# A two-layer hybrid encoder on one core: norm weights written as rows, norms turned two blocks at a time, and other places for the last MLP weights

## The chip, the core and the metric

The kernel runs on one core of a Trainium2 chip. The metric is the device time of one execution in microseconds; the median of three runs of the kernel before is 1523.51 us (1521.68 to 1525.11). One execution was profiled: it took 1525.2 us, with a span of 1523.4 us and a mean granted TensorE clock of 0.97. The engines are called as in the profile: PE (TensorE), DVE (VectorE), ACT (ScalarE), POOL (GpSimd), and SP, which here only issues DMAs.

## The reference

Two layers work on `x` of 512 x 1024 float32. Each layer mixes the tokens, then applies an MLP, both between two norms. Six vectors per layer (`shift`, `scale`, `gate`, twice) come from one vector `c` by a product with 1024 x 6144 weights:

```python
mod = (cond @ mod_w + mod_b)[:, None, :]
shift1, scale1, gate1, shift2, scale2, gate2 = jnp.split(mod, 6, axis=-1)
h = rms_norm(x, attn_pre_g) * (1.0 + scale1) + shift1
proj = h @ w_in
...
y = jnp.concatenate([y_a, y_b, y_c, y_d], axis=-1) @ w_out
x = x + gate1 * rms_norm(y, attn_post_g)
h = rms_norm(x, mlp_pre_g) * (1.0 + scale2) + shift2
y = jnp.square(jax.nn.relu(h @ mlp_w1)) @ mlp_w2
return x + gate2 * rms_norm(y, mlp_post_g)
```

The mixers (sparse attention, retention, gated linear attention, differential attention) are not touched by the change.

## The kernel before

**Products.** Each product of two matrices is made of three matmuls (`mm3`, L267 to L271): operands are split in a high part, rounded, and a low part, the rest. `prep` (L255 to L266) does so for a tile of weights: a DMA on SP's queue loads 256 KB into one of four `raw` buffers (L261), ACT casts the high part `whi` (L263), and DVE or POOL subtracts for the low part `wlo` (L265). Strings in the table `PLAN` say which of the two does it, letter by letter (`d` or `p`): `blo` for the first three weight groups of layer 1, `wolo` for the out-projection's, `w1lo` for the MLP's first hidden weights. `slots` is a list of pools that take the tiles in turn.

**Order.** The program is written as one stream; a scheduler sorts the instructions of each engine, and each engine then works in its order. A DMA waits in the order of the queue that issues it.

**Modulation vectors.** `gemv` (L279 to L282) loads 512 KB into one of two `gw` buffers by SP's queue and lets DVE multiply and sum them (1.2 us). Those of the MLP part of layer 0 and all of layer 1 (56 steps) are spread over the MLP of layer 0 by `fill`: one with each hidden tile, two with each output tile. `gain` (L304) makes of such a vector the 128 x 8 weights of a norm. The norms behind the projections need them as a row that is the same on all 128 partitions: `gain_row` (L488 to L495) writes the 128 x 8 tile to memory in the order of a row, four bytes at a time (L493, `rows<-g_post`), and reads it back to all partitions (L494, `row_post<-rows`), both on SP's queue. There are four such rows in the program.

**Rest of a layer** (`rest`, L1236 to L1363). Tokens go in four blocks of 128. The out-projection does 48 matmuls for each block (`po`); then `add_block` (L497) multiplies by the row, takes the mean of squares (`rsqrt_mean`, L467 to L483: two ACT squares, five short DVE steps, two short ACT steps) and updates x; `norm_block` (L505) norms the new x with another mean and two ACT multiplications (L511); and `turn_block` (L514 to L529) turns the normed block: eight PE transposes (L522) into two PSUM buffers, eight ACT evictions of 128x128 that apply scale and shift (L525), the cast `h_h` (L527), and on DVE the low part `h_l` (L528). The turn of a block stands behind the matmuls of the next one; that of block 3 behind the fourth hidden tile of the MLP. The MLP runs in four quarters q: eight hidden tiles `pf` of 24 matmuls (in q = 0 in two halves of 256 tokens each), squared into `hd` by `hidden` (ACT, DVE, a cast and a low part), then eight output tiles `p` of 24 matmuls. In the last quarter the output runs block by block, both halves of a block in a row, and each block is then added, normed and turned for the next layer.

**Transition.** The first weight groups of layer 1 (groups 3, 0 and 1, each of four tiles; L751 to L768) are applied block by block: `ptm` matmuls, of group 3 first; blocks 0 and 1 can go while blocks 2 and 3 are still normed, and `ch()`, the turn of block 3, is called at group 1 of block 1. ACT copies the results out of PSUM (`tK`, `Va`, `wi`, `ca`, L720 to L723; `tI`, L746). The four blocks of x are saved by DMAs of ACT's queue (L1347) and read back in the next out-projection.

Of the kernel before, what the change touches and what calls it, by code (L numbers as in the profile page):

```python
# [24 lines left out]
 'blo': 'dppd',  # L25
# [53 lines left out]
 'w1lo': 'dp',  # L79
 'wm': 12,  # L80
 'wolo': 'pdpddppp',
# [117 lines left out]
def tile_trunk(ctx: ExitStack, tc: tile.TileContext, a, out, dbg=None):  # L199
# [55 lines left out]
    def prep(src, shape, lo_eng=None):  # L255
        n = cnt[0]
        cnt[0] += 1
        pl, th, tl, bufs = slots[0]
        slots.append(slots.pop(0))
        raw = wp.tile(shape, F32, name=f"raw{n}", tag="raw", bufs=PLAN["rb"])  # L260
        sp.dma_start(raw, src)  # L261
        hi = pl.tile(shape, F32R, name=f"whi{n}", tag=th, bufs=bufs)
        act.copy(hi, raw)  # L263
        lo = pl.tile(shape, F32R, name=f"wlo{n}", tag=tl, bufs=bufs)
# [202 lines left out]
    def rsqrt_mean(halves, name):  # L467

        ss = tiny("ss" + name, 2)
        for c in range(2):  # L470
            junk = nt.tile([P, T], F32, name=f"jk{name}{c}", tag="nm_r", bufs=1)
            act.activation(junk, halves[c], AF.Square, accum_out=ss[:, c:c + 1])
# [32 lines left out]
    def norm_block(x, name):  # L505

        r = rsqrt_mean([x[:, hs(c)] for c in range(2)], name)
        xn = []
        for c in range(2):
            xn.append(nt.tile([P, T], F32, name=f"xn{name}{c}", tag="rs", bufs=RS))  # L510
            act.mul(xn[c], x[:, hs(c)], r)  # L511
        return xn
# [873 lines left out]
```

## Time and profile before

| | |
|---|---|
| median of three runs | 1523.51 us (1521.68 to 1525.11) |
| the profiled execution | 1525.2 us, span 1523.4 us |
| mixers of layer 0, out-projection, MLP, transition | to about 335, 390, 782, 833 us of the span |
| mixers of layer 1, out-projection, MLP | to about 1095, 1150, 1516 us |
| from the last matmul to the end | 7.6 us |
| DMA packets, and of these under 512 B | 83,094 and 13,188 |

Times are counted from the start of the span. A row of the timeline has its start, its length, engine, line, operation and output<-input; in brackets stands how long the engine was idle before it and what it waited for. A row of the waits has the waiting engine and line, the engine and line waited for, the total in us, how often, and the longest. A row of stretches has start:end, the width, and busy us of PE, its weight loads, DVE, ACT and POOL with their instructions, then the granted clock of TensorE, the DMA share and GB/s. A group's row has the instructions, busy us and mean ns, and the idle time ahead of them.

### The profile page before, as it was taken

How to read it: one execution, taken by the hardware profiler on the slowest of the kernel's cores; microseconds unless marked ns; L12 is line 12 of the kernel's file. 1: busy time of each engine (PE TensorE's matmuls, PEld its weight loads, DVE VectorE, ACT ScalarE, POOL GpSimd, SP SyncE). 2: the span in 40 equal slices, each digit the busy share in tenths (PEclk: the TensorE clock that was granted, in tenths of full speed). 3: DMA queues.
4: the chain of work that ended last, by engine and by line, in shares of the span. 5: the costliest groups of instructions: out<-in, count | busy, mean ns of one | idle time of the engine just before them, and what ended most of it. 6: DMA issues, size and time to landing. Idle time of an engine off the chain costs nothing.

```text
span 1523.4 us, 21884 instructions
## 1 busy us (share of the span) xinstructions
PE 1420.2 (93%) x7730; PEld 1148.0 (75%) x7730; DVE 947.6 (62%) x2119; ACT 759.0 (50%) x1739; POOL 250.7 (16%) x234
## 2 busy tenths in 40 slices
PE   8889889998899959999978989999988999999998
PEld 4576868766898838888868868787568988888886
DVE  8898978774674766525464989764555434254444
ACT  4577476565742312414465765856657444142331
POOL 3343421332100000000022344213330000000000
PEclk8999999999999969999999999999999999999999
DMA  9531222453287876524132102211331443142311
GB/s 345 189 93 42 84 70 84 147 185 112 64 278 192 276 214 206 131 63 125 56 117 71 37 28 78 76 43 42 120 113 59 111 123 93 62 130 82 107 42 56
DMA packets 83094, 173.13 MB, mean 114 GB/s; under 512 B 13188, under 2 KB 15910, under 8 KB 82728
## 3 DMA queue, kind: packets, MB, share of 16 engines
q1 hardware_dynamic: 82084, 169.59, 36.7%
q10 hardware_dynamic: 900, 2.14, 0.4%
q8 instruction: 61, 1.00, 0.3%
q14 instruction: 49, 0.40, 0.1%
HBM read 167.48 MB, written 4.21 MB: 113 GB/s over the span
## 4 chain that ended last, share of the span: by engine, by line
PE 70%; DVE 15%; ACT 6%; issue 4%; DMA 4%; POOL 1%; SPq 0%; ACTq 0%; DVEq 0%; POOLq 0%
PE p L271 8%; PE p L269 8%; PE p L270 8%; PE pf L269 7%; PE pf L270 7%; PE pf L271 7%; PE ptm L269 3%; PE ptm L270 3%; PE ptm L271 3%; DMA gw<-modw 3%; DVE ia L814 2%; DVE m L813 2%; ACT whi L263 1%; DVE ia L800 1%; PE ptc_t L271 1%
## 5 line engine op out<-in xcount | busy, mean ns | idle before, releaser
L263 ACT CAST whi<-raw 128x512 fp32r<-128x512 f32 x388 | 236.5, 621 | 336.6 <-PE p L271 120.7
L265 POOL TENSOR_TENSOR wlo<-raw,whi 128x512 fp32r<-128x512 f32 x122 | 161.3, 1342 | 751.8 <-ACT whi L263 707.5
L265 DVE TENSOR_TENSOR wlo<-raw,whi 128x512 fp32r<-128x512 f32 x266 | 184.0, 703 | 150.3 <-ACT whi L263 147.0
L270 PE MATMUL pf<-h_l,whi 128*128 128x512 f32 (+1 forms) x640 | 223.3, 349 | 0.0
L269 PE MATMUL pf<-h_h,whi 128*128 128x512 f32 (+1 forms) x640 | 223.3, 351 | 0.0
L271 PE MATMUL pf<-h_h,wlo 128*128 128x512 f32 (+1 forms) x640 | 223.0, 349 | 0.0
L269 PE MATMUL ptm<-whi,h_h 128*128 128x256 f32 x592 | 176.7, 299 | 10.0 <-ACT ca L723 6.8
L270 PE MATMUL ptm<-wlo,h_h 128*128 128x256 f32 x592 | 173.3, 293 | 0.9 <-POOL wlo L265 0.9
L271 PE MATMUL ptm<-whi,h_l 128*128 128x256 f32 x592 | 172.3, 291 | 0.0
L282 DVE CUSTOM_DVE_ANT_0 gw<-gw,cond 128x1024 f32<-128x1024 f32 x80 | 101.6, 1273 | 65.2 <-DMA gw<-modw 64.9
L269 PEld LDWEIGHTS pf<-h_h,whi 128*128 128x128 f32 x640 | 121.4, 191 | 16.9 <-ACT h_h L527 0.2
L271 PEld LDWEIGHTS pf<-h_h,wlo 128*128 128x128 f32 x640 | 121.1, 189 | 16.8
L270 PEld LDWEIGHTS pf<-h_l,whi 128*128 128x128 f32 x640 | 121.1, 189 | 16.7
L269 PEld LDWEIGHTS ptm<-whi,h_h 128*128 128x128 f32 x592 | 116.1, 196 | 18.4 <-issue 7.3
L270 PEld LDWEIGHTS ptm<-wlo,h_h 128*128 128x128 f32 x592 | 116.7, 197 | 6.3 <-issue 4.8
L271 PEld LDWEIGHTS ptm<-whi,h_l 128*128 128x128 f32 x592 | 116.5, 197 | 1.8 <-issue 1.5
L270 PE MATMUL po<-wlo,yT_h 128*128 128x512 f32 x128 | 51.8, 404 | 2.9 <-POOL wlo L265 2.9
L813 DVE MAX8 m<-ia 128x8 f32<-128x256 f32 (+2 forms) x96 | 53.2, 555 | 1.3
L269 PE MATMUL po<-whi,yT_h 128*128 128x512 f32 x128 | 52.8, 412 | 0.2 <-ACT yT_h L446 0.2
L814 DVE MATCH_REPLACE8 ia<-m,ia 128x256 f32<-128x256 f32 (+2 forms) x96 | 51.9, 541 | 0.0
L271 PE MATMUL po<-whi,yT_l 128*128 128x512 f32 x128 | 51.2, 400 | 0.6 <-DVE yT_l L447 0.6
L917 ACT COPY QF<-q 32x256 f32<-32x256 f32 x120 | 48.4, 403 | 5.2 <-DVE q L894 2.2
(418 smaller groups left out, 3028.4 us busy)
## 6 DMA issues: line engine op xcount, KB each, us to landing
raw<-w SPq DMA_DIRECT2D x256, 256.0 KB, 2.8
gw<-modw SPq DMA_DIRECT2D x80, 512.0 KB, 4.3
raw<-wtm SPq DMA_DIRECT2D x76, 256.0 KB, 2.8
gs<-modw SPq DMA_DIRECT2D x16, 512.0 KB, 7.5
raw<-wo SPq DMA_DIRECT2D x32, 256.0 KB, 2.8
raw<-wtc SPq DMA_DIRECT2D x24, 256.0 KB, 2.8
xin<-xT SPq DMA_DIRECT2D x8, 256.0 KB, 3.5
wq<-wtm SPq DMA_DIRECT2D x8, 256.0 KB, 5.7
```

The costliest lines, as they stand in the source:

```text
L263: act.copy(hi, raw)
L265: (lo_eng or dve).tensor_tensor(lo, raw, bits(hi), ALU.subtract)
L269: pe.matmul(ps, l[0], r[0], start=start, stop=False)
L270: pe.matmul(ps, l[0], r[1], start=False, stop=False)
L271: pe.matmul(ps, l[1], r[0], start=False, stop=stop)
L282: return dve.tensor_tensor_reduce(raw, raw, cond, 1.0, 0.0, ALU.mult, ALU.add, modT[l][:, c:c + 1])
L800: e.scalar_tensor_tensor(t, rl, wi[:, b, hd:hd + 1], t, ALU.mult, ALU.add)
L813: dve.max(m8, acc)
L814: dve.match_replace(acc, m8, acc, MARK)
L917: f(Q[r, :, hd, :], QS4[c // 2][r, 2 * (c % 2):2 * (c % 2) + 2, :])
```

## The change

Four things change.

1. **Rows.** The weights of the norm behind a projection are made as soon as their modulation vector is there (`gain_out`): PE turns the 128 x 8 tile to 8 x 128, ACT copies it out of PSUM, and a DMA of POOL's queue writes it as eight contiguous pieces. The read to all partitions, and the saves of x, also go to POOL's queue.
2. **Norms and turns.** x is normed by one ACT square of 128x1024 and one DVE scaling of 128x1024, written in the place of the block's output tile. Two blocks are turned at once (`turn_half`): 4 x 4 transposes, evictions of 128x256, by turns ACT's and DVE's. Blocks 0 and 1 are turned behind the first half of block 3's out-projection, blocks 2 and 3 behind the sixth hidden tile. In the last quarter of layer 0 the output runs (0,0), (0,1), (1,0), (1,1), (2,1), (3,1), then the turn of blocks 0 and 1, then (2,0), (3,0), each a block and a half of the columns; the turn of blocks 2 and 3 is called at group 1 of block 1, as block 3's was.
3. **Weights.** Of the last MLP weights the eight of the second half of the columns (`wr`) lie in the place of the MLP's input `h2`, which is read until the last hidden tile. The first weights of layer 1 take other slots.
4. **Low parts.** `blo`, `w1lo` and `wolo` give more of them to DVE: 34 of POOL's 122 in the program, 14 in each out-projection and its MLP's start, 6 at the transition.

```diff
- 'blo': 'dppd',
+ 'blo': 'dddd',
- 'w1lo': 'dp',
+ 'w1lo': 'd',
- 'wolo': 'pdpddppp',
+ 'wolo': 'ppdddddd',
...
+                    if part in (2, 5):
+                        gain_out(l, "post1" if part == 2 else "post2")
...
+    def gain_out(l, which):
+        gain(l, which)
+        pt = tr.tile([P, T], F32, name=f"tg_{which}{l}", tag="tr")[0:KT, 0:P]
+        pe.transpose(pt, gmul[l, which], ident)
+        g = nt.tile([P, T], F32, name=f"gt_{which}{l}", tag="sq")[0:KT, 0:P]
+        act.copy(g, pt)
+        pool.dma_start(rows[2 * l + (which == "post2")], g)
     def gain_row(l, which):
-        sp.dma_start(d.rearrange("k p -> p k"), g)
-        sp.dma_start(row, d.rearrange("k p -> (k p)").unsqueeze(0).broadcast_to([P, DM]))
+        pool.dma_start(row, d.rearrange("k p -> (k p)").unsqueeze(0).broadcast_to([P, DM]))
...
+    def norm_block(x, xn, name):
+        ss = tiny("ss" + name)
+        f = xn.rearrange("p c t -> p (c t)")
+        square(ss, x, f)
+        dve.tensor_scalar(f, x, rsqrt_mean(ss, name), None, ALU.mult)
+        return f
+    def turn_half(l, which, sh_part, hf, xn, parts, name):
...
+        for c in range(4):
...
+            for i in range(2):
+                for b in range(2):
+                    k = 2 * c + i
+                    pe.transpose(pt[:, i, P * b:P * b + P], xn[2 * hf + b][:, P * k:P * k + P], ident)
+            for i in range(2):
+                k = 2 * c + i
+                if i:
+                    act.activation(v[:, i], pt[:, i], AF.Identity, scale=g[:, k:k + 1], bias=sh[:, k:k + 1])
+                else:
+                    dve.tensor_scalar(v[:, i], pt[:, i], g[:, k:k + 1], sh[:, k:k + 1], ALU.mult, ALU.add)
...
-            if b:
-                turn(b - 1)
+                if (b, c) == (NB - 1, 0):
+                    turn(0)
...
-                    if (q, half, f) == (0, 0, 3):
-                        turn(NB - 1)
+                    if (q, half, f) == (0, 0, 5):
+                        turn(1)
...
+        wr = h_tiles(f"wr{l}_")
+        ws = [[prep(a["w2"][l, 3, 0, k], [P, T]) for k in range(KT)],
+              [prep(a["w2"][l, 3, 1, k], [P, T], place=wr[k]) for k in range(KT)]]
+        last = [(0, 0), (0, 1), (1, 0), (1, 1)]
+        last += [(2, 1), (3, 1), (2, 0), (3, 0)] if l + 1 < L else [(2, 0), (2, 1), (3, 0), (3, 1)]
...
-                act.dma_start(xsave[b], x)
-                xn[b] = norm_block(x, f"p1n{l}_{b}")
+                pool.dma_start(xsave[b], x)
+                xn[b] = norm_block(x, y[b], f"p1n{l}_{b}")
```

How the order moves, at three places. On TensorE, at the end of layer 0's out-projection, the order before has the last matmuls of block 3 (`po_3_1`), the first four transposes of block 2 (`txp_20`) and then the MLP's first hidden tiles (`pf`):

```order
L270 MATMUL po_3_1_4395<-wlo_4041,yT_h 128x512
L271 MATMUL po_3_1_4395<-whi_4039,yT_l 128x512
L522 MATMUL txp_20_4420<-ident,xnpn_20_4366 128x128 x4
L269 MATMUL pf_0_0_0_4510<-h_h,whi_4500 128x256
L269 MATMUL pf_0_1_0_4552<-h_h,whi_4542 128x256
```

With the change the transposes of blocks 0 and 1 (`txp_00` to `txp_03`, out of the output tile `yo_m`) stand between the halves of block 3:

```order
L274 MATMUL po_3_0_4304<-whi_3993,yT_l 128x512
L538 MATMUL txp_00_4329<-ident,yo_m 128x128 x4
L538 MATMUL txp_01_4339<-ident,yo_m 128x128 x4
L272 MATMUL po_3_1_4369<-whi_3999,yT_h 128x512
L273 MATMUL po_3_1_4369<-wlo_4000,yT_h 128x512
L274 MATMUL po_3_1_4369<-whi_3999,yT_l 128x512
L272 MATMUL po_3_1_4369<-whi_4005,yT_h 128x512
L273 MATMUL po_3_1_4369<-wlo_4006,yT_h 128x512
L274 MATMUL po_3_1_4369<-whi_4005,yT_l 128x512
L538 MATMUL txp_02_4349<-ident,yo_m 128x128 x4
```

So the transposes of a block that was just normed are gone from there, and no transpose stands between the out-projection and the first hidden tiles. On SP's queue, in the MLP of layer 0, the order before has the write of a row among the loads of MLP weights (`raw<-w`) and modulation weights (`gw`):

```order
L261 DMA raw_6023<-w 128x512
L280 DMA gw_3_2_6117<-modw 128x1024
L261 DMA raw_6029<-w 128x512
L493 DMA rows<-g_post_11548 128x8x1
L280 DMA gw_3_3_6120<-modw 128x1024
L261 DMA raw_6035<-w 128x512
```

With the change the same loads follow one another:

```order
L259 DMA raw_6001<-w 128x512
L283 DMA gw_3_2_6089<-modw 128x1024
L259 DMA raw_6007<-w 128x512
L283 DMA gw_3_3_6092<-modw 128x1024
L259 DMA raw_6013<-w 128x512
```

The write has gone to POOL's queue, behind a transpose and a copy. On ACT, at the transition, the order before has block 3's normed halves (`xnp1n_30`, `xnp1n_31`) ahead of the copies of group 3's result for block 0 (`Va`, `wi`, `ca` out of `ptm_3_0`):

```order
L478 ACTIVATE rsp1n_3_7784<-rsp1n_3_7784 128x1
L263 CAST whi_7864<-raw_7862 128x512
L263 CAST whi_7870<-raw_7868 128x512
L720 COPY tK_0_7884<-ptm_3_0_7892 128x128
L511 ACTIVATE xnp1n_30_7791<-x_3_4046,rsp1n_3_7784 128x512
L511 ACTIVATE xnp1n_31_7793<-x_3_4046,rsp1n_3_7784 128x512
L721 COPY Va_7880<-ptm_3_0_7892 128x64
L722 ACTIVATE wi_7881<-ptm_3_0_7892 128x8
L723 COPY ca_7882<-ptm_3_0_7892 128x16
```

With the change these copies, of blocks 0 and 1, come ahead of block 3's square (`ym_1_5060, ssp1n_3`):

```order
L739 COPY tK_0_7788<-ptm_3_0_7796 128x128
L740 COPY Va_7784<-ptm_3_0_7796 128x64
L267 CAST whi_7750<-raw_7748 128x512
L741 ACTIVATE wi_7785<-ptm_3_0_7796 128x8
L742 COPY ca_7786<-ptm_3_0_7796 128x16
L267 CAST whi_7756<-raw_7754 128x512
L739 COPY tK_1_7789<-ptm_3_1_7825 128x128
L740 COPY Va_7784<-ptm_3_1_7825 128x64
L741 ACTIVATE wi_7785<-ptm_3_1_7825 128x8
L742 COPY ca_7786<-ptm_3_1_7825 128x16
L473 ACTIVATE ym_1_5060,ssp1n_3_7689<-x_3_4048 128x1024
```

The first casts of those weights have moved too, behind block 2's square (`ym_0_5059, ssp1n_2`):

```order
L473 ACTIVATE ym_0_5059,ssp1n_2_7628<-x_2_4047 128x1024
L267 CAST whi_7714<-raw_7712 128x512
L480 ACTIVATE rsp1n_2_7632<-msp1n_2_7630 128x1
L267 CAST whi_7720<-raw_7718 128x512
L481 ACTIVATE rsp1n_2_7632<-rsp1n_2_7632 128x1
```

`whi_7714` is the first of the twelve tiles that the projections of blocks 0 and 1 need.

More of the change, by code (lines that the diff above doesn't have):

```diff
@@ L465, in tiny, with square, rsqrt_mean @@
         return nt.tile([P, 2], F32, name=name, tag="tn", bufs=8)[:, :n]
[L467 to L472, printed above, removed]
+    def square(ss, src, junk):
+        act.activation(junk, src, AF.Square, accum_out=ss)
+    def rsqrt_mean(ss, name):
         m = tiny("ms" + name)
-        dve.tensor_tensor(m, ss[:, 0:1], ss[:, 1:2], ALU.add)
-        dve.tensor_scalar(m, m, 1.0 / DM, EPS, ALU.mult, ALU.add)
+        dve.tensor_scalar(m, ss, 1.0 / DM, EPS, ALU.mult, ALU.add)
         r = tiny("rs" + name)
@@ L500, in add_block @@
             dve.tensor_tensor(ys[c], src[c], row[:, hs(c)], ALU.mult)
-        r = rsqrt_mean(src, name)
+        s1 = tiny("sa" + name)
+        dve.tensor_tensor(s1, ss[:, 0:1], ss[:, 1:2], ALU.add)
+        r = rsqrt_mean(s1, name)
         for c in range(2):
             dve.scalar_tensor_tensor(x[:, hs(c)], ys[c], r, x[:, hs(c)], ALU.mult, ALU.add)
[L505 to L512, printed above, removed]
@@ L570, in y_tiles @@
         m = yb.tile([P, 4, T], F32, name=f"{name}_m", tag="ym", bufs=1)
-        o = [yb.tile([P, T], F32, name=f"{name}_{i}", tag="y", bufs=4) for i in range(4)]
-        return o[:2] + [m[:, i, :] for i in range(4)] + o[2:], m
+        o = [yb.tile([P, 2, T], F32, name=f"{name}_{i}", tag="y", bufs=2) for i in range(2)]
+        return [o[0][:, i] for i in range(2)] + [m[:, i, :] for i in range(4)] + [o[1][:, i] for i in range(2)], m
     E = {"p": pool, "d": dve}
@@ L705, in run @@
                 proj_tc(h, w.pop(g), l, g, evict)
-        slots[:] = [(wp, "whi", "wlo", WB), (s0, "zh", "zl", 8 if l else 6)]
+        slots[:] = [(s0, "zh", "zl", 10)] * 10 + [(wp, "whi", "wlo", WB)] * 2
         if l:
@@ L1334, in rest @@
-        ws = [[prep(a["w2"][l, 3, c, k], [P, T]) for k in range(KT)] for c in range(2)]
-        for b in range(NB):
-            for c in range(2):
-                ps = acc(f"p2{l}_3_{b}_{c}", T)
-                for k in range(KT):
-                    mm3(ps, (hid[k][0][:, tb(b)], hid[k][1][:, tb(b)]), ws[c][k], k == 0, k == KT - 1)
-                dve.tensor_tensor(y[b][c], y[b][c], ps, ALU.add)
-            if turn and b:
-                turn(b - 1)
-            x = X["x"][b]
-            gy = [nt.tile([P, T], F32, name=f"gy{l}_{b}{c}", tag="rs", bufs=RS) for c in range(2)]
-            add_block(x, y[b], gy, row, f"p2{l}_{b}")
-            if turn:
-                act.dma_start(xsave[b], x)
-                xn[b] = norm_block(x, f"p1n{l}_{b}")
-            else:
-                for c in range(2):
-                    sp.dma_start(out[b][:, hs(c)], x[:, hs(c)])
@@ L1352, in rest @@
-        ch = (lambda: turn(NB - 1)) if turn else None
+        wr = h_tiles(f"wr{l}_")
[3 more added lines that the diff above has]
+        last += [(2, 1), (3, 1), (2, 0), (3, 0)] if l + 1 < L else [(2, 0), (2, 1), (3, 0), (3, 1)]
+        seen = set()
+        turn = None
+        for b, c in last:
+            if l + 1 < L and (b, c) == (2, 0):
+                gain(l + 1, "pre1")
+                h = h_tiles(f"h1{l + 1}_")
+                parts = whole[f"h1{l + 1}_"]
+                turn = lambda hf: turn_half(l + 1, "pre1", 0, hf, xn, parts, f"p1{l}_{hf}")
+                turn(0)
+            ps = acc(f"p2{l}_3_{b}_{c}", T)
+            for k in range(KT):
+                mm3(ps, (hid[k][0][:, tb(b)], hid[k][1][:, tb(b)]), ws[c][k], k == 0, k == KT - 1)
+            dve.tensor_tensor(y[b][:, c], y[b][:, c], ps, ALU.add)
+            if b not in seen:
+                seen.add(b)
+                continue
+            x = X["x"][b]
+            gy = [nt.tile([P, T], F32, name=f"gy{l}_{b}{i}", tag="rs", bufs=RS) for i in range(2)]
+            add_block(x, [y[b][:, i] for i in range(2)], gy, row, junk(f"p2{l}_{b}"), f"p2{l}_{b}")
+            if l + 1 < L:
+                pool.dma_start(xsave[b], x)
+                xn[b] = norm_block(x, y[b], f"p1n{l}_{b}")
+            else:
+                for i in range(2):
+                    sp.dma_start(out[b][:, hs(i)], x[:, hs(i)])
@@ L1355, in rest @@
             X["pool"].close()
-        return h, ch
+        return h, turn
     h, ch = h_tiles("h10_"), None
```

60 lines of the change are left out of this document (26 added, 34 removed).

## The prediction, as put on record

> **What bounds the kernel now.** I read the page's first part, then the table by stretches of time, then the waits of TensorE, and only then the rows around each wait. The page says that TensorE (PE) is the busy one:
>
> ```profile
> span 1523.4 us, 21884 instructions
> PE 1420.2 (93%) x7730; PEld 1148.0 (75%) x7730; DVE 947.6 (62%) x2119; ACT 759.0 (50%) x1739; POOL 250.7 (16%) x234
> ```
>
> So 103 us of the span have no matmul. The change removes hardly any matmul work, so it can gain only there, and where the granted clock is low. The table by stretches (start:end, width, busy time of each engine, granted clock, DMA share, GB/s) tells where that is:
>
> ```profile
> 335.00:375.00 40.00, 35.79 (x147) 27.44 (x146) 22.74 (x43) 23.82 (x59) 13.16 (x10) 0.96 0.54 167
> 375.00:410.00 35.00, 30.12 (x191) 27.20 (x190) 19.77 (x43) 24.16 (x64) 5.11 (x4) 0.95 0.21 61
> 500.00:600.00 100.00, 81.40 (x324) 62.61 (x323) 69.30 (x119) 27.90 (x49) 0.00 (x0) 0.88 0.80 244
> 600.00:750.00 150.00, 150.00 (x647) 121.23 (x646) 69.50 (x112) 50.98 (x90) 0.00 (x0) 1.00 0.36 99
> 780.00:830.00 50.00, 38.34 (x275) 36.66 (x274) 25.47 (x60) 29.14 (x85) 13.60 (x12) 0.90 0.34 101
> 1095.00:1170.00 75.00, 65.48 (x329) 53.80 (x328) 41.37 (x85) 46.93 (x121) 18.15 (x14) 0.93 0.40 120
> ```
>
> From 600 to 750 TensorE never stops. Four places are left that the change touches: the out-projection of layer 0 (idle 4.21 + 4.88 = 9.1 us), the MLP of layer 0 at 500 to 600 (18.6), the transition to layer 1 at 780 to 830 (11.7) and the out-projection of layer 1 (9.5). The waits of TensorE (total, times, longest) name the releasers:
>
> ```profile
> PE txp L522 <- ACT vxp L525: 9.8, 2, 4.9
> PE txp L522 <- ACT xnpn L511: 5.1, 2, 2.6
> PE po L270 <- POOL wlo L265: 2.9, 8, 0.6
> PE p L271 <- DVE hd_4l L447: 7.1, 1, 7.1
> PE ptm L269 <- ACT ca L723: 6.8, 1, 6.8
> PE ptm L269 <- ACT whi L263: 3.2, 1, 3.2
> ```
>
> The first three come twice, once a layer: 4.9 + 2.55 + 1.45 = 8.9 us per out-projection. The one of `hd_4l` opens the MLP's stall, and the rest of its 18.6 us are the hidden tiles behind it; the two of `ptm` (10.0 us) are most of the transition's.
>
> **A and D: later turns in the two out-projections.** Before the change a block's eight transposes stand right behind the next block's matmuls on TensorE, block 2's ahead of the MLP's first tile; they wait for the block's norm or, where both PSUM buffers are full, for the evictions, and both are ACT's work. After each stall the clock is low:
>
> ```profile
> 363.20:368.20 5.00, 4.97 (x19) 4.34 (x20) 0.26 (x2) 4.08 (x11) 0.00 (x0) 0.68 0.23 70
> 393.70:398.00 4.30, 4.30 (x23) 4.12 (x24) 1.38 (x2) 4.30 (x12) 0.00 (x0) 0.60 0.00 0
> 397.42 0.28 PE L269 MATMUL pf<-h_h,whi 128*128 128x256 f32 x1
> 397.54 0.28 PE L270 MATMUL pf<-h_l,whi 128*128 128x256 f32 x1
> ```
>
> The low clock costs 5.0 x 0.32 + 4.3 x 0.40 = 3.3 us, so an out-projection loses about 9.1 + 3.3 = 12.4 us. After the change blocks 0 and 1 are turned behind the first half of block 3's matmuls, long after both are normed, and blocks 2 and 3 behind six hidden tiles: 6 x 24 matmuls, one each 0.12 us by the two rows above, are 17 us of cover (a matmul of 512 columns, twice as long, takes 0.24). What has to fit under it is block 3's chain, worked out from these groups of 335 to 410 (busy, mean ns, idle before; the row with a start time is block 3's scaling):
>
> ```profile
> L503 DVE SCALAR_TENSOR_TENSOR x<-yo,rspo,x 128x512 f32<-128x512 f32 x4 | 2.8, 749 | 0.1
> L481 DVE SCALAR_TENSOR_TENSOR ttpo<-ttpo,mspo 128x1 f32<-128x1 f32 x4 | 2.8, 692 | 0.1
> L482 DVE SCALAR_TENSOR_TENSOR rspn<-ttpn,rspn 128x1 f32<-128x1 f32 x4 | 0.6, 159 | 0.1
> L511 ACT ACTIVATE xnpn<-x,rspn 128x512 f32<-128x512 f32 x8 | 5.3, 715 | 2.3 <-DVE rspn L482 2.2
> 406.17 1.34 ACT L511 ACTIVATE xnpn<-x,rspn 128x512 f32<-128x512 f32 x2 [0.61 <-DVE rspn L482]
> L265 POOL TENSOR_TENSOR wlo<-raw,whi 128x512 fp32r<-128x512 f32 x14 | 18.3, 1326 | 56.3 <-ACT whi L263 56.3
> L265 DVE TENSOR_TENSOR wlo<-raw,whi 128x512 fp32r<-128x512 f32 x12 | 8.2, 688 | 1.4 <-ACT whi L263 1.3
> ```
>
> Two squares (at most 1.4, taken like the scalings), two means whose five short steps on DVE and two on ACT I put at 1.5 each, two updates of x (1.5), one square of 128x1024 (at most 1.4) and one scaling of 128x1024 on DVE, which the trace lacks: between 0.75 (one update of x, of half the width) and 1.43 (two of today's scalings); I take 1.2, near the 1.23 of DVE's other 128x1024 operation in B. That makes about 9 us under 17. In the trace the same chain takes 18.7 us, from the end of its matmuls (4.9 us of stall ahead of the second window, so 388.8) to 407.5 (the row of 406.17); but there ACT does the evictions of blocks 1 and 2 in between, which now come earlier or later. If the cover failed, the 4.9 us would be back.
> The low parts that move from POOL to DVE are 14 per layer here by the strings (wolo 10 to 4, w1lo 8 to 0): 14 x 0.69 = 9.7 us more on DVE, which has 42.5 of 75 us now. It also takes half of the turn's evictions and the scaling (some 8 us), but the short operations go from 0.69 towards 0.16 when POOL is quiet. DVE would hold some 56 of 64 us: no bound, though without much room. ACT gets lighter. I leave 2 us for weights that come late and one short stall: A = 10.5, D = 10.5; ends 8 (a third of the stalls comes back) and 12.4.
>
> **B: the norm weights' write in the MLP of layer 0.** The first row is the norm weights' write of 526 to 545 (KB, us to landing), by the code in 1024 elements of 4 bytes; the others are DVE's waits for the modulation loads, over the run (total, times, longest) and one by one, and what TensorE does meanwhile:
>
> ```profile
> rows<-g_post SPq DMA_DIRECT2D x1, 4.0 KB, 12.0
> DVE gw L282 <- DMA gw<-modw: 64.9, 42, 6.9
> 464.30 1.22 DVE L282 CUSTOM_DVE_ANT_0 gw<-gw,cond 128x1024 f32<-128x1024 f32 x1 [6.90 <-DMA gw<-modw]
> 469.48 1.23 DVE L282 CUSTOM_DVE_ANT_0 gw<-gw,cond 128x1024 f32<-128x1024 f32 x1 [3.94 <-DMA gw<-modw]
> 473.77 1.23 DVE L282 CUSTOM_DVE_ANT_0 gw<-gw,cond 128x1024 f32<-128x1024 f32 x1 [2.87 <-DMA gw<-modw]
> 541.40 1.23 DVE L282 CUSTOM_DVE_ANT_0 gw<-gw,cond 128x1024 f32<-128x1024 f32 x1 [6.66 <-DMA gw<-modw]
> 542.55 0.69 DVE L447 TENSOR_TENSOR hd_4l<-rf,hd_4h 128x512 fp32r<-128x512 f32 x1
> 531.76 0.39 PE L269 MATMUL p<-whi,hd_0h 128*128 128x512 f32 x1
> 535.00:565.00 30.00, 11.66 (x24) 6.55 (x25) 19.39 (x32) 6.95 (x13) 0.00 (x0) 0.60 0.80 228
> ```
>
> The write takes 12 us for 4 KB, and the load of the modulation weights (`gw`) beside and behind it keeps DVE idle for 6.66 us; DVE does its work in order, so the hidden tile `hd_4l` waits for it. TensorE wants that tile 12 matmuls behind 531.76, at about 534.6, and gets it at 543.2. Two writes have made DVE late by then: 6.9 + 3.9 + 2.9 us less some 0.4 each (12.5), and 6.7. Without them `hd_4l` would come near 524, ahead of its need, and the tiles behind it follow their own matmuls. Gross: 18.6 us idle and 11.7 x 0.40 = 4.7 us of low clock, 23 in all. The new write is 8 rows of 512 B instead of 1024 elements, on POOL's queue, behind one transpose and one small ACT copy; SP's loads are no longer behind it. I take 17 and not 23, since DVE also waits for `gw` loads with no such write near (42 waits, 64.9 us; the four above are 20.4 of them), and since the moved low parts make DVE busier ahead of this place; ends 7 (only the second write's 6.7) and 23.
>
> **C: the transition.**
>
> ```profile
> 781.70 0.40 PE L271 MATMUL p<-whi,hd_7l 128*128 128x512 f32 x1
> 799.95 1.33 ACT L511 ACTIVATE xnp1n<-x,rsp1n 128x512 f32<-128x512 f32 x2 [1.93 <-DVE rsp1n L482]
> 790.00:795.00 5.00, 4.82 (x29) 4.62 (x28) 4.45 (x6) 1.46 (x4) 2.75 (x2) 0.69 0.73 210
> 801.60:806.60 5.00, 5.00 (x23) 4.86 (x24) 2.08 (x9) 2.25 (x10) 0.00 (x0) 0.50 0.31 94
> 832.59 0.37 ACT L746 COPY tI<-ptm 128x256 f32<-128x256 f32 x1
> ```
>
> Waits of 10.0 us and low clock 4.8 x 0.31 + 5.0 x 0.50 = 4.0 us make 14. The 6.8 us wait (`ca`) is ACT's: it does block 3's scaling at 799.95, and the copies that free PSUM only behind it. That scaling goes to DVE, the order puts those copies ahead of block 3's square, and half 0 is turned before the last 48 matmuls (11 us) of the MLP. What is late next: the first cast of the projection's weights stands behind block 2's square, so it comes some 1.5 us behind the last MLP matmul, where two of them were ready before; and the last block's norm, whose chain of 9 us leaves its turn at about 12 us with the queueing, under 17 us of projections of blocks 0 and 1. Counted forward the last copy `tI` falls about 40 us behind the last MLP matmul instead of 50.9 (832.59 less 781.70). I take 9 of the 14; ends 3 and 13.
>
> **Small additions.** The second half of the last MLP weights can be cast only when the last hidden matmul has read the tile in whose place they go. The 24 matmuls of the first half (24 x 0.24 = 5.8 us) cover eight casts and low parts (0.7 us each); only four raw buffers are loaded ahead. I take 1 us a layer, 0 to 3. Four transposes and copies of the norm weights: under 0.5 us. The saves of x leave ACT's queue for POOL's and are read 300 us later: nothing.
> One rule of the Trainium skill speaks against the move to POOL's queue. The rows first: short DVE operations take 0.692 us beside POOL's work instead of 0.159, so POOL and DVE do hold each other up here. The page "SBUF — State Buffer", section "Who interferes with whom", says that GpSimd must write the descriptors of a DMA on its queue, and that a DVE operation in a two-port mode locks it out for its whole length. By that page's 0.62 against 3.1 us a transfer would come about 2.5 us later, an estimate; for 12 transfers all on the path that would be 30 us and the sum 1509. I keep the sum: by the rows no reader of these transfers is that near.
>
> **Sum.** 10.5 + 10.5 + 17 + 9 - 2.5 = 44.5 us. The profiled execution took 1525.2 us (span 1523.4 and 1.8 around it), which gives 1480.7; the median of the runs is 1.7 lower, so **1479 us**.
>
> **Rivals.** (1) The modulation loads stay late: the rate is set by the other loads (DMA share 0.80 at 500 to 600), and only the 6.7 us of one write come back, so B is 7: 1489. For it: `gw` waits of 1 to 3 us between the writes. Against it: four of DVE's 42 waits for `gw`, all behind the two writes, hold 20.4 of the 64.9 us. (2) The transition's gain is lost: 12 weights have to be cast and loaded through four raw buffers after the MLP's end, behind block 2 and 3's norms on ACT, so C is 0: 1488. For it: two casts were ahead before and none is now. (3) Slower: DMAs issued by POOL hold DVE, as POOL's subtractions hold its short operations now (0.692 against 0.159 us). Place: the 4 writes, 4 row reads and 4 saves, each with DVE work behind it that someone waits for. If each held DVE as long as its transfer lasts now (writes 12.0; reads 4.3, and I give the saves of the same size as much), that is 4 x 20.6 = 82 us, and 1479 + 82 = 1561. It decides from 44.5 / 12 = 3.7 us for each on the path:
>
> ```profile
> row_post<-rows SPq DMA_DIRECT2D x4, 512.0 KB, 4.3
> ```
>
> Against it: most lie in the MLP, where DVE is idle a third of the time (30.7 of 100 us at 500 to 600). The lock that the Trainium skill tells of on its page "SBUF — State Buffer" would work in this way too, but no run here shows a DMA on POOL's queue. That the write does not get shorter is case 1.
>
> **Chances.** Forecast 0.65 (its own range 1468 to 1490, from the ends of the four terms taken as independent), rival 1 0.15, rival 2 0.12, rival 3 0.05, and 0.03 for a gain under 3 us. Both 1 and 2 together give 1498. The range of 1466 to 1499 leaves out rival 3 and the outer ends of the others. Faster by over 0.2% (3 us, what a measurement of this kernel can tell): 0.92; within: 0.03; slower: 0.05.
>
> **What would show it.** Right: no wait of a transpose for ACT in the out-projections; TensorE without idle from 335 to 410 but for 2 us; no wait for `hd_4l`; about 4000 fewer packets under 512 B (4 x 1024 elements); the last `tI` copy some 40 us behind the last MLP matmul. Wrong: waits for `hd` tiles stay; TensorE waits for `whi` or `wr` at the MLP's end; short DVE operations grow around POOL's DMAs.

## The result and the profile after

The changed kernel takes 1484.82 us (median of four runs, 1482.21 to 1486.54) where the kernel before took 1522.6 us beside it: ratio 0.9753, 95% interval 0.9726 to 0.978. That is 37.8 us less; 44.5 were forecast, and 1484.8 lies in the range. The profiled executions lie 43.0 us apart (spans 1523.4 and 1480.4), since that of before was its longest run and that of after its shortest. One execution of the run before_mix below took 2720.7 us, for a reason that is not known; it is left out of that run's ratio.

First the head of the page after, and its DMA line:

```profile
span 1480.4 us, 21794 instructions
PE 1408.6 (95%) x7734; PEld 1138.1 (77%) x7734; DVE 962.9 (65%) x2177; ACT 722.8 (49%) x1623; POOL 213.2 (14%) x212
DMA packets 79063, 173.13 MB, mean 117 GB/s; under 512 B 9125, under 2 KB 11879, under 8 KB 78697
```

There are 4063 fewer packets under 512 B (13188 before), which is about the four writes of 1024 elements. TensorE is idle for 72 us instead of 103. The stretches that answer to those of before:

```profile
335.00:410.00 75.00, 73.29 (x421) 62.37 (x420) 54.30 (x123) 44.45 (x104) 0.00 (x0) 1.00 0.38 120
520.00:600.00 80.00, 74.01 (x302) 57.92 (x302) 55.53 (x95) 22.71 (x40) 0.52 (x1) 0.94 0.67 223
740.00:800.00 60.00, 53.07 (x356) 46.55 (x355) 35.75 (x98) 32.02 (x91) 8.67 (x10) 1.00 0.32 103
1060.00:1140.00 80.00, 77.67 (x453) 65.78 (x452) 57.01 (x128) 46.50 (x108) 0.60 (x1) 1.00 0.37 119
```

The out-projections run at full clock with 1.7 and 2.3 us idle; 6 us are left at 520 to 600, 6.9 at the transition. The waits of TensorE name what is left:

```profile
PE thA L679 <- DVE hlA L675: 5.0, 2, 3.6
PE p L272 <- ACT hd_7h L451: 3.7, 1, 3.7
PE p L274 <- DVE hd_6l L452: 1.2, 1, 1.2
PE p L272 <- ACT hd_6h L451: 1.1, 1, 1.1
PE ptm L272 <- ACT ca L742: 1.5, 1, 1.5
PE ptm L272 <- ACT whi L267: 1.2, 1, 1.2
```

No transpose waits for ACT's evictions or scalings; `hd_4l` is gone, later hidden tiles are not; the wait for `ca` went from 6.8 to 1.5. New is `thA`, in the first mixers, at 5.0 instead of 2.0.

The stages, worked out in each trace from the first and last matmul of each (us; E is the end of the last MLP matmul of layer 0, `tI` the start of the last of the six `tI` copies behind it):

| | mixers 0 | out-proj. 0, to the first `pf` | to outputs of quarter 1 | outputs of quarter 1 | to the end E of MLP 0 | E to last `tI` | E to out-proj. 1 | out-proj. 1, to `pf` | MLP 1 | tail |
|---|---|---|---|---|---|---|---|---|---|---|
| before | 335.0 | 59.5 | 137.3 | 70.1 | 180.3 | 50.5 | 312.0 | 60.5 | 361.2 | 7.6 |
| after | 337.8 | 47.6 | 137.2 | 55.0 | 180.4 | 42.5 | 305.7 | 48.6 | 360.7 | 7.4 |

So A = 11.9 (10.5 forecast), B = 15.1 (17), C = 8.0 to the last `tI` and 6.3 to the next out-projection (9), D = 11.9 (10.5). Against these stand 2.8 us in the first mixers; the last MLP weights in their new place cost nothing (180.4 and 360.7).

### The profile page after: what moved, and what is told of

It reads as the page before. It is cut to its first block, busy times and chain, and to the rows that moved or that the text cites. A ratio compares the mean times of both kernels' runs of the same rounds, so it can differ in the third digit from the quotient of the medians.

```text
span 1480.4 us, 21794 instructions
## 1 busy us (share of the span) xinstructions
PE 1408.6 (95%) x7734; PEld 1138.1 (77%) x7734; DVE 962.9 (65%) x2177; ACT 722.8 (49%) x1623; POOL 213.2 (14%) x212
## 4 chain that ended last, share of the span: by engine, by line
PE 65%; DVE 16%; DMA 9%; ACT 5%; issue 4%; POOL 1%; SPq 0%; DVEq 0%; ACTq 0%; POOLq 0%
PE p L272 7%; PE p L274 7%; PE p L273 7%; PE pf L273 7%; PE pf L274 7%; PE pf L272 6%; DMA gw<-modw 5%; DVE ia L833 3%; PE ptm L272 2%; PE ptm L273 2%; PE ptm L274 2%; DVE m L832 2%; DMA raw<-w 2%; PE po L272 2%; PE po L274 1%
## 5 line engine op out<-in xcount | busy, mean ns | idle before, releaser
L267 ACT CAST whi<-raw 128x512 fp32r<-128x512 f32 x372 | 227.5, 621 | 304.6 <-PE p L274 118.2
L268 DVE TENSOR_TENSOR wlo<-raw,whi 128x512 fp32r<-128x512 f32 x284 | 196.2, 704 | 138.2 <-ACT whi L267 135.3
L268 POOL TENSOR_TENSOR wlo<-raw,whi 128x512 fp32r<-128x512 f32 x88 | 117.1, 1351 | 230.8 <-ACT whi L267 196.7
L285 DVE CUSTOM_DVE_ANT_0 gw<-gw,cond 128x1024 f32<-128x1024 f32 x80 | 101.4, 1270 | 47.7 <-DMA gw<-modw 47.5
L1312 DVE TENSOR_TENSOR rf<-rf,pf 128x512 f32<-128x512 f32 (+1 forms) x80 | 45.9, 575 | 35.3 <-ACT rf L1311 35.3
L1311 ACT ACTIVATE rf<-pf 128x512 f32<-128x512 f32 (+1 forms) x80 | 40.6, 507 | 41.2 <-PE pf L274 41.2
```

Of the source, the lines that this page charges most:

```text
L268: (lo_eng or dve).tensor_tensor(lo, raw, bits(hi), ALU.subtract)
L285: return dve.tensor_tensor_reduce(raw, raw, cond, 1.0, 0.0, ALU.mult, ALU.add, modT[l][:, c:c + 1])
L1311: act.activation(rl, ps, AF.Relu)
L1312: dve.tensor_tensor(rl, rl, ps, ALU.mult)
```

## The experiments

The stages of all twelve runs, in the same way, with the median time (the changed kernel's is 1484.8, the kernel before's 1522.6 to 1524.0 beside them):

| | us | mixers 0 | out 0 | to q1 | q1 outputs | E to `tI` | E to out 1 | out 1 |
|---|---|---|---|---|---|---|---|---|
| rows_back | 1492.8 | 333.1 | 48.8 | 137.2 | 67.3 | 43.3 | 304.3 | 49.0 |
| rows_only | 1512.0 | 339.1 | 58.2 | 137.5 | 54.2 | 49.4 | 310.9 | 60.6 |
| turn_early | 1484.8 | 336.9 | 48.7 | 137.4 | 56.9 | 44.0 | 305.6 | 49.4 |
| spread | 1474.4 | 340.3 | 47.8 | 138.9 | 45.2 | 43.7 | 305.9 | 48.7 |
| own_gt | 1477.8 | 332.5 | 47.7 | 137.3 | 56.3 | 42.8 | 303.9 | 48.7 |
| act_turn | 1486.4 | 338.7 | 49.2 | 137.2 | 57.5 | 44.9 | 308.4 | 49.5 |
| lo_back | 1497.3 | 336.9 | 51.3 | 137.9 | 56.6 | 46.1 | 311.3 | 52.4 |
| plain_last | 1482.7 | 338.9 | 47.4 | 137.2 | 55.2 | 42.0 | 305.1 | 49.8 |
| best | 1471.4 | 332.1 | 49.4 | 139.7 | 45.2 | 43.3 | 307.3 | 47.7 |
| best_hw | 1473.0 | 332.4 | 48.5 | 140.0 | 45.2 | 44.3 | 305.4 | 47.7 |
| forced_early | 1539.2 | 337.6 | 73.7 | 135.8 | 58.6 | 44.5 | 307.6 | 75.4 |
| before_mix | 1471.1 | 333.1 | 52.2 | 138.2 | 45.1 | 40.3 | 300.2 | 51.8 |

A stage's time differs by one or two us between runs of the same code, as the column of the transition shows in kernels that are alike there.

**The rows: rows_back and rows_only.**

```diff
-                    if part in (2, 5):
-                        gain_out(l, "post1" if part == 2 else "post2")
...
-        pool.dma_start(row, d.rearrange("k p -> (k p)").unsqueeze(0).broadcast_to([P, DM]))
+        sp.dma_start(d.rearrange("k p -> p k"), gmul[l, which])
+        sp.dma_start(row, d.rearrange("k p -> (k p)").unsqueeze(0).broadcast_to([P, DM]))
```

> The changed kernel, but the norm weights are again written in single elements by SP's queue and read back on SP's queue, at the old place in the program; all else stays. Theory of the prediction (the element-wise write holds the modulation loads up, and so DVE and the hidden tiles): the first outputs of quarter 1 in layer 0's MLP take about 70 us again instead of 55, so some 15 us more than the changed kernel, about 1500 us. Rival (the stall is the pace of the modulation loads, two for each hidden tile on DVE, whatever the write): 0 to 7 us more, 1485 to 1492. Beside it: if the early transposes and copies of the norm weights are what makes the first mixers 2.8 us longer after the change (TensorE starts the out-projection at 337.8 instead of 335.0), that start moves back to 335 here, and the total is 3 us lower than said.

(The calls of `gain` that this needs again are not shown.) The other way round, the kernel before with `gain_out` and POOL's queue for the rows, all else as it was:

> The kernel before with the rows alone: norm weights turned on TensorE, copied by ACT and written contiguously by POOL's queue; norms, turns, last weights and low parts as before. Theory: 15 us less than before, about 1508 us, with the outputs of quarter 1 at about 55 us instead of 70. Rival (pace of the modulation loads): at most 7 less, 1516 or more.

Taken back, the write costs 8.0 us in the median (ratio to before 0.9801, 0.9782 to 0.982, against 0.9753) and 12.3 in its stage; put in alone it brings 11.2 us (0.9932, 0.9915 to 0.9948) and 15.9 in its stage. The theory's stage is nearly right, and both totals are some 4 us off in the same way: the first mixers are 4.7 us shorter without `gain_out` (333.1 against 337.8) and 4.1 longer with it (339.1 against 335.0). In the waits of rows_back the old stall is there again:

```profile
PE p L274 <- DVE hd_4l L450: 6.0, 1, 6.0
PE p L272 <- ACT hd_6h L449: 3.8, 1, 3.8
```

**The cost in the first mixers: own_gt.** The trace after, at the first of the four writes (start, length, engine, line, operation, tiles, idle before and releaser; the last row is TensorE's):

```profile
213.51 0.75 POOL L498 DMA_DIRECT2D rows<-gt_post  x1
216.29 0.19 DVE L583 TENSOR_TENSOR r2A<-tA,ssA 128x32 f32<-128x32 f32 x1 [2.08 <-DMA rows<-gt_post]
218.01 0.63 PE L679 MATMUL thA<-ident,hlA 128*128 128x128 f32 x4 [3.62 <-DVE hlA L675]
```

A rotary step has nothing to do with norm weights. But its scratch tile `r2A` and ACT's copy `gt_post` share the two buffers of one tag, so it must wait until the DMA has read the copy. If that is so, another buffer takes the wait away; if POOL held DVE, it would not.

```diff
-        g = nt.tile([P, T], F32, name=f"gt_{which}{l}", tag="sq")[0:KT, 0:P]
+        g = nt.tile([P, T], F32, name=f"gt_{which}{l}", tag="nm_r", bufs=1)[0:KT, 0:P]
```

> The changed kernel with one name changed: ACT's copy of the norm weights, which POOL's queue writes out, lies in another scratch buffer (that of the norms' squares) instead of one of the two that the rotary embeddings use too. Theory (in the first mixers a rotary step of DVE waits 2.1 us for that write to read its buffer, TensorE's transposes wait 3.6 us behind it, and so the out-projection starts at 337 to 340 us instead of 333 to 335): the wait goes, the out-projection starts 3 to 4 us earlier, the total falls by as much to about 1481. Rival (DVE is held by POOL writing the descriptors of the DMA, whatever the buffer): the wait stays, no change, 1484.8.

1477.8 us (0.9705, 0.969 to 0.9719). The same step of DVE, and TensorE's waits in the first 335 us:

```profile
210.96 0.19 DVE L583 TENSOR_TENSOR r2A<-tA,ssA 128x32 f32<-128x32 f32 x1
```

```profile
PE thA L679 <- DVE hlA L675: 2.1, 2, 1.4
```

The wait is gone and the out-projection starts at 332.5. Over the runs above, the eight with the shared buffer start it at 336.9 to 340.3, the six without at 332.1 to 335.0. The theory holds; its size was 3 to 4 us and is 5 to 7.

**What is left at quarter 1: spread.** In the trace after the low parts of the last hidden tiles of quarter 1 run on DVE at these times:

```profile
518.28 0.69 DVE L452 TENSOR_TENSOR hd_4l<-rf,hd_4h 128x512 fp32r<-128x512 f32 x1
...
519.49 1.22 DVE L285 CUSTOM_DVE_ANT_0 gw<-gw,cond 128x1024 f32<-128x1024 f32 x1
...
522.17 1.23 DVE L285 CUSTOM_DVE_ANT_0 gw<-gw,cond 128x1024 f32<-128x1024 f32 x1 [0.26 <-DMA gw<-modw]
...
523.32 0.69 DVE L452 TENSOR_TENSOR hd_5l<-rf,hd_5h 128x512 fp32r<-128x512 f32 x1
...
529.24 0.69 DVE L452 TENSOR_TENSOR hd_6l<-rf,hd_6h 128x512 fp32r<-128x512 f32 x1
...
534.82 0.68 DVE L452 TENSOR_TENSOR hd_7l<-rf,hd_7h 128x512 fp32r<-128x512 f32 x1
```

Two modulation steps (`gw`) stand ahead of each tile, some 2.7 us apart, so a tile comes every 5.0 to 5.9 us, and DVE is late since the quarter before: TensorE starts the outputs at 522.6. The edit ties each step behind the low part of one hidden tile (or, not shown, the sum of one output tile), and calls one with each tile from quarter 0 on: 56 steps for 56 tiles.

```diff
-                    fill(1 if q else 0)
+                    fill(1)
...
-                        fill(2)
+                        fill(1)
...
-            split(rl, hid[0][:, c], hid[1][:, c])
+            fence[:] = [split(rl, hid[0][:, c], hid[1][:, c])]
```

> The changed kernel with the modulation steps of layer 0's MLP spread evenly: one with each hidden tile and each output tile from the first quarter on, each held behind that tile's low part on DVE (a tie of order, no other work). Theory: what is left of the stall at quarter 1 (outputs 55 us where 45 are matmul time) is DVE's order, in which two modulation steps of 2.8 us stand ahead of each hidden tile; then it goes, and the time falls by 8 to 10 us to about 1476. Rival (the memory traffic is the limit at 250 to 280 GB/s): 0 to 3 us less, 1482 to 1485.

1474.4 us (0.9681, 0.9665 to 0.9697), and the outputs of quarter 1 take 45.2 us, the time of their matmuls. The stretch of 520 to 600, where 6 us were idle:

```profile
520.00:600.00 80.00, 80.00 (x345) 64.24 (x344) 48.30 (x82) 24.34 (x42) 0.52 (x1) 1.00 0.57 185
```

TensorE does not stop. But the stretch moves 185 GB/s instead of 223, since steps have moved out of it, so it does not by itself tell the order from the memory's rate. How late the hidden tiles of quarter 1 are tells more. Their low parts start 9.0 us (the first tile) to 12.0 us (the last) behind the tile's last matmul in the changed kernel, and 2.4 to 2.5 us in spread. Two rows of DVE's waits in the changed kernel, from 433 to 478 (the outputs of the quarter before) and from 478 to 535.5:

```profile
DVE gw L285 <- DMA gw<-modw: 16.3, 12, 3.1
DVE gw L285 <- DMA gw<-modw: 9.2, 12, 1.5
```

So late loads have a part in making DVE late, in the quarter before. In quarter 1 it stays late by its order: with two steps ahead of each tile it does not catch up.

**The place of the turns: turn_early and forced_early.** The first calls the turns earlier:

```diff
+            if b % 2:
+                turn(b // 2)
...
-                if (b, c) == (NB - 1, 0):
-                    turn(0)
...
-                    if (q, half, f) == (0, 0, 5):
-                        turn(1)
```

> The changed kernel, but in both out-projections the turns of two blocks are called right behind block 1 and right behind block 3, as early as they can be, instead of half a block and six hidden tiles later. Theory (the place is what counts: the transposes wait for a norm that was just begun): a stall of 5 to 8 us and the low clock behind it return in each layer, 14 to 20 us in all, 1499 to 1505 us. Rival (the relief of ACT counts, by wider evictions shared with DVE and the scaling on DVE): 0 to 5 us more, 1485 to 1490.

1484.83 us (0.9746, 0.9731 to 0.976), as the changed kernel. That looks like the rival, but it was no test of the place: in the order of this kernel the scheduler had left two of a turn's sixteen transposes at the early place and put the other fourteen later by itself, by 7 us in the first turn and 8 in the second. The second run forces the place by a tie from each transpose to the next six groups of matmuls:

```diff
+        if start:
+            for x in tp:
+                after(x[0], m)
+                x[1] -= 1
+            tp[:] = [x for x in tp if x[1]]
```

> The changed kernel with the turns of the two out-projections called right behind block 1 and right behind block 3, and ties of order that hold the next six groups of matmuls behind all their transposes (without such ties the scheduler had put most transposes back where they can run). Theory of the prediction (the place is what takes the stall away; a block's chain of add and norm takes about 9 us): each of the four turns stalls TensorE 8 to 11 us, with 1.7 us of low clock behind each; an out-projection takes 68 to 72 us instead of 47.6, and the total is 1525 to 1535. Rival (the pieces are what counts, the place is not): under 3 us a turn, below 1497.

1539.2 us (1.01, 1.0082 to 1.0117), slower than before the change. TensorE's waits:

```profile
PE txp L545 <- DVE yo L531: 14.6, 2, 7.3
PE txp L545 <- DVE yo_m L531: 14.1, 3, 7.0
PE txp L545 <- ACT vxp L551: 8.5, 6, 3.1
```

Four turns wait about 7 us each for the block's scaling and up to 3.1 for evictions; an out-projection takes 26 to 27 us more, which is beyond the theory's range. The place counts: right behind its block a turn stalls here. With fourteen of its transposes 7 to 8 us later, as in turn_early, it does not.

**Smaller pieces, and who does them: act_turn.**

```diff
-                if i:
+                if True:
                     act.activation(v[:, i], pt[:, i], AF.Identity, scale=g[:, k:k + 1], bias=sh[:, k:k + 1])
...
-        dve.tensor_scalar(f, x, rsqrt_mean(ss, name), None, ALU.mult)
+        act.mul(f, x, rsqrt_mean(ss, name))
```

> The changed kernel with ACT doing all evictions of the turns (128x256) and the scaling of the norm (128x1024), as it did before the change in smaller pieces; places of the turns as in the change. Theory formed on the run with early turns (ACT's load at these places is what counts: the evictions shared with DVE and the scaling on DVE took the stalls away, not the place): the out-projections take 3 to 6 us more each, the transition 3 to 5, about 1495 in all. Rival (two blocks at a time, in larger pieces, is enough): under 3 us more in all, 1485 to 1488.

1486.4 us (0.9744, 0.9721 to 0.9766): 1.6 and 0.9 us more in the out-projections and 2.4 to `tI`, in a profiled execution that was its slowest. The median is the rival's; the difference from the changed kernel's time is within the spread of either.

**The low parts: lo_back.** Only the three strings go back.

```diff
- 'blo': 'dddd',
+ 'blo': 'dppd',
- 'w1lo': 'd',
+ 'w1lo': 'dp',
- 'wolo': 'ppdddddd',
+ 'wolo': 'pdpddppp',
```

> The changed kernel with the three strings of low parts as before: 34 more of them on POOL. Theory of the prediction (POOL's slow subtractions make TensorE wait for wo's low parts and stretch DVE's short operations): 2 to 4 us more in each out-projection and 2 at the transition, about 1492. Rival (their place is covered): 0 to 2 us, 1485 to 1487.

1497.3 us (0.9834, 0.9821 to 0.9847), 12.5 more than the changed kernel: 3.7 and 3.8 in the out-projections, 3.6 to `tI` and 5.6 to the next out-projection. The out-projections are as the theory had them, the transition and the total are beyond it. TensorE waits in this kernel's first out-projection for two things that are not in the changed kernel's waits there:

```profile
PE txp L538 <- ACT vxp L542: 1.5, 1, 1.5
PE po L273 <- POOL wlo L268: 1.0, 3, 0.4
```

DVE's short steps of the mean in the out-projection, of this kernel and then of the changed one (busy, mean ns, idle before):

```profile
L484 DVE SCALAR_TENSOR_TENSOR ttpo<-ttpo,mspo 128x1 f32<-128x1 f32 x4 | 2.8, 691 | 0.1
L483 DVE TENSOR_TENSOR ttpo<-rspo 128x1 f32<-128x1 f32 x4 | 2.1, 534 | 1.5 <-ACT rspo L481 1.5
```

```profile
L484 DVE SCALAR_TENSOR_TENSOR ttpo<-ttpo,mspo 128x1 f32<-128x1 f32 x4 | 0.6, 160 | 0.1
L483 DVE TENSOR_TENSOR ttpo<-rspo 128x1 f32<-128x1 f32 x4 | 0.6, 155 | 1.0 <-ACT rspo L481 1.0
```

Over the whole trace of lo_back 14 of DVE's 110 steps of these two kinds on 128x1 overlap a subtraction on POOL and take 1.14 us on the average; the other 96 take 0.16. In the changed kernel none overlaps one.

**The order of the last outputs: plain_last.** The weights `wr` go back to ordinary slots (not shown), and layer 0 ends block by block.

```diff
-        last += [(2, 1), (3, 1), (2, 0), (3, 0)] if l + 1 < L else [(2, 0), (2, 1), (3, 0), (3, 1)]
+        last += [(2, 0), (2, 1), (3, 0), (3, 1)]
...
-            if l + 1 < L and (b, c) == (2, 0):
+            if l + 1 < L and (b, c) == (3, 0):
```

> The changed kernel with the last MLP weights in the slots of before and, in layer 0, the last outputs block by block, so that blocks 0 and 1 are turned ahead of block 3's 48 matmuls instead of ahead of the last 48 of blocks 2 and 3. Theory of the prediction (the gain at the transition is the copies ahead of block 3's norm and DVE's scaling, which stay here; but block 2's norm is done 5.6 us earlier, and casts of the next weights stand earlier): the transition takes 40 to 44 us as in the change, total within 3 us of it, 1482 to 1488. Rival (the column order is what brings it): the transition is back at 48 to 50 us, 1491 to 1493.

1482.7 us (0.9741, 0.9724 to 0.9758), `tI` at 42.0 instead of 42.5: no difference that can be told. The half of the last weights in the MLP input's place brings nothing here and costs nothing.

**Both mends, and the queue: best and best_hw.** The two edits of spread and own_gt together:

> The changed kernel with both mends: modulation steps spread with the ties of order, and ACT's copy of the norm weights in the scratch buffer of the squares. Theory: the two gains lie in different stages (first mixers, about 5 us in the profile and 7 in the median; outputs of quarter 1, about 10) and add up: 1484.8 - 7.0 - 10.4 = 1467.4. Rival (they share a cause, since both ease DVE's waits): 1472 to 1475.

and with the rows on SP's queue and the saves on ACT's:

```diff
-        pool.dma_start(rows[2 * l + (which == "post2")], g)
+        sp.dma_start(rows[2 * l + (which == "post2")], g)
...
-                pool.dma_start(xsave[b], x)
+                act.dma_start(xsave[b], x)
```

> As the kernel with both mends, but the writes and reads of the norm weights' rows are issued by SP's queue and the saves of x by ACT's, and none by POOL's. Theory of the prediction (no reader of these transfers is near, so the queue does not matter, and DVE is not held): within 2 us of the kernel with both mends, 1466 to 1470. Rival, the rule that the Trainium skill states on its page SBUF — State Buffer (descriptors written by POOL wait for DVE, and hold it): 3 to 8 us less, 1460 to 1465. A second rival (SP's queue stands still while the write waits for ACT's copy, and loads behind it come late): 3 to 8 us more, 1470 to 1476.

1471.4 us (0.9655, 0.9636 to 0.9673) and 1473.0 (0.9666, 0.9648 to 0.9684). The first lies between the theory's 1467.4 and the rival's 1472 to 1475: the gains add but for 4 us, of which the stages show 2.5 on the way to quarter 1 and 1.8 in the first out-projection. The queue makes no difference that can be told, and neither rival shows: the stages up to quarter 1's outputs differ by less than 1 us, and the total is 1.6 us more, within the spread of either, and not 3 to 8 more or less. The rule of the Trainium skill's page "SBUF — State Buffer", section "Who interferes with whom", that DVE can hold up POOL's writing of a DMA's descriptors, may hold, but no stage here shows anything that waits for it.

**The kernel before with two small edits: before_mix.** The strings of the change, and the spreading, and nothing else: the element-wise write, the turns and norms stay as before.

> The kernel before with two edits that act in different stages: the three strings of low parts as in the change, and the modulation steps spread with ties of order; the norm weights are still written element by element, norms and turns stay as before. Strings: in the changed kernel taking them back cost 3.7 us in each out-projection and 3.6 to 5.6 from the transition on; if that adds up here, the out-projection falls from 59.5 to about 56 and the total by 11 to 13. Rival (the gain is tied to the new turns): under 1 us for each. Spreading: theory (the write only hurts because DVE is late already) outputs of quarter 1 take 45 to 50 us instead of 70; rival (the write alone stalls them) 58 to 70. Total by both theories 1488 to 1492, by both rivals 1512 to 1523.

1471.1 us (0.9655, 0.9637 to 0.9672), 13.7 us faster than the changed kernel, better than both theories together, and as fast as best (1471.4). So once the low parts and the steps are in order, rows, norms, turns and weight places bring nothing to the total. The stretch of 500 to 600, in which 18.6 us were idle, and the waits at the out-projection (335 to 410) and the transition (740 to 810):

```profile
500.00:600.00 100.00, 100.00 (x433) 80.88 (x432) 64.11 (x107) 34.21 (x58) 0.00 (x0) 1.00 0.62 200
```

```profile
PE txp L522 <- ACT vxp L525: 3.3, 1, 3.3
PE txp L522 <- ACT xnpn L511: 0.9, 1, 0.9
```

```profile
PE ptm L269 <- ACT whi L263: 1.4, 1, 1.4
PE ptm L269 <- ACT ca L723: 0.4, 1, 0.4
```

The spreading moved neither the out-projections nor the transition of the changed kernel (run spread: 47.8, 48.7 and 305.9 for 47.6, 48.6 and 305.7), so what changes there is put down to the strings. They take 7.3 and 8.7 us, and 11.8 out of the time from E to the next out-projection. The element-wise write, issued at 450.0, still keeps DVE waiting for the loads behind it:

```profile
464.13 1.23 DVE L282 CUSTOM_DVE_ANT_0 gw<-gw,cond 128x1024 f32<-128x1024 f32 x1 [5.83 <-DMA gw<-modw]
```

But TensorE does not stall. The first hidden tile of quarter 1 is 8.1 us late here, by the measure used for spread, and with one step ahead of each tile DVE catches up: the sixth is 2.4 us late. In rows_back, with the same write and two steps, the tiles are 17.0 to 25.3 us late.

## Why the prediction was right, and where it was not

**The sum** was 44.5 for 37.8 measured (43.0 between the profiled spans). Its four large terms came out at 11.9, 15.1, 8.0 and 11.9 for 10.5, 17, 9 and 10.5. Each is near, but that is in part luck: A, C and D hold a gain of the strings of which the prediction priced only the 1.45 us a layer that TensorE waited for POOL's low parts.

**A and D, size right, cause half named.** The place of the turns counts, as forced_early shows. The chain under the cover of 17 us was put at about 9 us and is 11.8 in the changed kernel, from block 3's last matmul to the end of its scaling, so the cover held with less to spare:

```profile
384.45 0.40 PE L274 MATMUL po<-whi,yT_l 128*128 128x512 f32 x1
395.87 0.75 DVE L524 TENSOR_SCALAR yo<-x,rspn 128x1024 f32<-128x1024 f32 x1
```

But the step "14 x 0.69 = 9.7 us more on DVE" was put down as a risk only. Taking the strings back costs 3.7 us an out-projection, and without the new turns they bring 7.3 and 8.7. With POOL silent DVE's short steps, which the chain passes one by one, take 0.16 us instead of 0.69, and the chains of blocks 0 to 2 take 11.9, 8.0 and 9.9 us where lo_back has 14.2, 9.8 and 11.2 (block 3: 11.8 and 11.4). TensorE's wait for POOL's low parts (1.45 us a layer before) is gone too; which of the two weighs more was not tried. The prediction had both rows and priced only the second.

**B, size right, the cause lies deeper.** The write did what the prediction said: 12.3 us taken back, 15.9 alone. But it could do so only because DVE was late already, with two modulation steps ahead of each hidden tile; with the steps spread DVE catches up behind the same write (before_mix). The step "`hd_4l` would come near 524" had the first tile right (it ran at 518.3), and "the tiles behind it follow their own matmuls" failed: they followed the modulation steps, at some 5.5 us each, and 9.9 us stayed. That is a part of rival 1: the loads do stay late. But its 7 us are refuted, and so is its reason as the whole of it, since the same loads, one to a tile, stall nothing (spread).

**C, size right, cause half right.** The wait for `ca` went as forecast, from 6.8 to 1.5 us, and with the order that was named: `ca` of block 0 is copied 9.8 us behind the last MLP matmul, ahead of block 3's square at 11.4, where before it came at 19.3, behind block 3's scaling. But the premise "That scaling goes to DVE" was not needed. In before_mix ACT still does the scaling, and the copies of blocks 0 and 1 stand ahead of block 3's first square there too:

```profile
758.44 0.21 ACT L723 COPY ca<-ptm 128x16 f32<-128x16 f32 x1
758.83 0.25 ACT L723 COPY ca<-ptm 128x16 f32<-128x16 f32 x1
760.09 0.64 ACT L472 ACTIVATE jkp1n<-x 128x512 f32<-128x512 f32 x1
765.65 1.34 ACT L511 ACTIVATE xnp1n<-x,rsp1n 128x512 f32<-128x512 f32 x2 [0.21 <-DVE rsp1n L482]
```

Its transition is the shortest of all (40.3). And lo_back, which has the scaling on DVE and block 0's copies as early (9.3), gains 4.4 us to `tI` but only 0.7 to the next out-projection. So much of the gain comes with the string `blo`, six low parts that left POOL, which the prediction did not price here: taking the strings back costs 3.6 of the 8.0 us to `tI` and 5.6 of the 6.3. Whether they work through the order, through POOL's slower subtractions ahead of the matmuls or through DVE's short steps is not shown. The order of the last outputs brought nothing (plain_last). Rival 2 was wrong: the wait for the casts is 1.2 us where it was 3.2.

**Small additions, wrong both ways.** The last weights were put at 1 us a layer and cost nothing. "Four transposes and copies of the norm weights: under 0.5 us" missed 5 us: the instructions are short, but the copy holds a buffer until a DMA has read it, and another stage needs that buffer.

**Rival 3** did not come: POOL spends 0.52 to 0.75 us on an issue, and other queues for the same transfers change nothing. The one DVE step that did wait for a DMA of POOL's waited for a buffer.

**Open.** From E to the next out-projection before_mix takes 300.2 us, the kernels with the new norms and turns and the same strings 303.9 to 308.4. So the norms, turns and rows together win 4.6 and 3.2 us in the changed kernel's out-projections over before_mix, and lose 5.5 from E to the next out-projection and 4.7 in the first mixers, the latter mended by own_gt; why the 5.5, no run tells. The strings and the spreading were not run apart from each other in the kernel before, so their shares are read from the stages. A kernel with the new out-projection and the old transition was not tried, nor were the new pieces at the old places, so what place and pieces bring in A and D is not told apart.

## What to carry to other kernels

Before a chain of short steps is moved or covered, look at what stretches the steps: here three strings that moved 34 subtractions from one engine to another were worth 12.5 of the 37.8 us. An engine that works in order makes every optional job a toll for the work behind it, so spread the jobs evenly and tie them behind that work; here a slow transfer then stalled nothing. A tile that a DMA reads belongs in a buffer that no hot stage rotates through.

## What the runs showed of the hardware

The new scaling and evictions on DVE, in the out-projection of the changed kernel:

```profile
L524 DVE TENSOR_SCALAR yo_m<-x,rspn 128x1024 f32<-128x1024 f32 x2 | 1.5, 754 | 0.1
L544 DVE TENSOR_SCALAR vxp<-txp,g_pre,modT 128x256 f32<-128x256 f32 x8 | 4.1, 537 | 0.2
```

A scaling of 1024 elements from buffer to buffer takes 0.754 us, less than was taken (1.2) and at the low end of its bounds, while an eviction of a quarter of that out of PSUM takes 0.537. The write of the norm weights in eight pieces lands in 2.5 to 4.9 us from POOL's queue, where that in 1024 elements took 11.1 to 12.0 from SP's:

```profile
L498 POOL DMA_DIRECT2D rows<-gt_post x4: 522/546/752, 213.5 to 645.5; - x4
DMA to landing us min/median/max: 2.5/3.0/4.9
```
